# The MLPs' first products as seven products of halves per pair of feature tiles

## The chip, the cores and the metric

The kernel runs on one core of a Trainium2 chip (trn2). The metric is the device time of one execution in microseconds (us), as the median of several runs on the same chip.

## The reference

A decoder trunk of two layers over 1024 tokens of 1024 features, in float32. Layer 0 mixes the tokens with an S5 state-space mixer and a gated linear unit (GLU), layer 1 with a Mamba-2 SSD mixer. After each mixer stands an MLP, which is what changes here. Cut to what matters:

```python
def _sq_relu_mlp(h, w1, w2):          # h [1024, 1024], w1 [1024, 4096], w2 [4096, 1024]
    a = jax.nn.relu(h @ w1)
    return (a * a) @ w2

for i in range(2):
    sh1, sc1, g1, sh2, sc2, g2 = split(silu(c) @ ada_w[i] + ada_b[i])
    x = x + g1 * mixer_i(_modulate(_rmsnorm(x, norm_mix_g[i]), sh1, sc1))
    h = _modulate(_rmsnorm(x, norm_mlp_g[i]), sh2, sc2)       # h * (1 + scale) + shift
    x = x + g2 * _sq_relu_mlp(h, mlp_w1[i], mlp_w2[i])
return _rmsnorm(x, final_norm_g)
```

## The kernel before

Activations lie with the features on the 128 partitions: `x` and `h` are 8 feature tiles of 1024 tokens, each in two halves of 512 tokens (`f` or `half` 0 and 1), so one matmul takes a 128 x 128 block of weights and 512 columns of tokens into one PSUM bank. Every float32 operand of a dense product is split into two parts that float32r holds exactly, `hi` and `lo` (`split`, L80: a cast on ACT, a subtraction on DVE), and a product is three matmuls, hi·hi, hi·lo and lo·hi (`mm3`, L98). A `unit` (L86) is a raw tile of weights of 128 x 1024, loaded by SP's queue, and its split into two stationary tiles; units rotate through a ring of five.

An MLP (`mlp`, L351) goes through the 4096 inner features in 8 groups (`fg`) of 4 feature tiles. In each group the first products are made for 4 tiles and 2 halves (`project`, 24 matmuls each, 192 in all), their squared relu is made by ACT and DVE and split into `ah` and `al`, and then the second products (`accumulate`, L377) run over the 4 tiles for 8 output tiles and 2 halves, 12 matmuls each, 192 in all. Their sums are added to `x`, times the gate, on DVE (L384). So the inner activations of a group never leave SBUF, and `x` stays there through the whole MLP. While layer 0's MLP runs, the modulation vectors of layer 1 are made on DVE, as dot products over 512 KB tiles (`mods`, L296), four steps for each half group.

The norm in front of the MLP works on one half of the tokens at a time (`norm_half`, L184): squares on ACT, their sum on DVE, the sum over partitions and the spreading of 1/rms on PE (L158, L141), then two DVE operations and one ACT operation for each feature tile (L194, L201, L202). The mixers end with the second half of the tokens (`glu` L737 and `ssd_out` L993 call `mid(f)`), so that the norm of the first half runs beside the mixer's matmuls of the second half, and the norm of the second half beside the MLP's products of the first half. In layer 0, `mid` of the MLP itself makes the norm for the SSD mixer, and writes `x` to DRAM (`rscr`).

The code is written out in one order. An instruction takes its place in its engine's queue when its inputs and its buffer are there, and of several such the one that stands first in the text. So work from further down can run ahead where an engine would be idle, if a buffer is free for it. Once the kernel is built, the order in each queue is fixed. Pools of tiles are allocated as two stacks, from the left and from the right; a pool that takes the place of a released one waits tile by tile for the old users.

Of the kernel before, what the change touches and what calls it, by code (L numbers as in the profile page):

```python
# [70 lines left out]
def psw(K):  # L71
    """A bank for the work of a mixer."""
    return K.pw.tile([P, 512], F32, tag="pw", name="pm")
# [6 lines left out]
def split(K, hi, lo, src):  # L80
    """src = hi + lo, each of them exact in float32r."""
    K.nc.scalar.copy(hi, src)  # L82
    K.nc.vector.tensor_tensor(lo, src, hi.bitcast(F32), op=ALU.subtract)  # L83


def unit(K, src, n=1024):  # L86
    """n columns of stationary blocks, split in two."""
    raw = K.raw.tile([P, 1024], F32, tag="raw", name="raw")[:, 0:n]
    K.nc.sync.dma_start(raw, src)
    K.wturn = (K.wturn + 1) % 5  # L90
    wt = K.wt if K.wturn < 2 or not K.wx else K.wx
# [6 lines left out]
def mm3(K, ps, terms, start=True, stop=True):  # L98
    """ps = sum of w^T x over the terms, w and x given as (hi, lo)."""
    n = len(terms)  # L100
    for i, (wh, wl, xh, xl) in enumerate(terms):
        K.nc.tensor.matmul(ps, wh, xh, start=start and i == 0, stop=False)  # L102
        K.nc.tensor.matmul(ps, wh, xl, start=False, stop=False)  # L103
        K.nc.tensor.matmul(ps, wl, xh, start=False, stop=stop and i == n - 1)  # L104
# [11 lines left out]
def rsqrt(K, y, v):  # L116
    """y = v ** -0.5 by Newton's steps from the bits of v."""
# [14 lines left out]
def pss(K):  # L132
    """A bank for the norms."""
# [3 lines left out]
def spread(K, y, bank=pss):  # L137
    """PSUM [P, 512] whose rows are all the 512 values of y [P tokens, 4 chunks]."""
# [6 lines left out]
def rstd_half(K, xs, bank=pss):  # L145
    """1/rms of each of 512 tokens, on all partitions."""
# [37 lines left out]
def norm_half(K, x, h, half, G, sh):  # L184
    """h = x * rstd * G + sh, split, for one half of the tokens."""
# [12 lines left out]
def shift_split(K, t, h, sh):  # L198
    """h = t + sh, split."""
# [5 lines left out]
def h_tile(K, k, half, s, dtype=F32R):  # L205
    """The slot of the h pool for (feature tile, half, hi or lo)."""
# [27 lines left out]
def together(main, other, ratio):  # L234
    """Runs the generator main to its end with ratio steps of the other after each of its own."""
# [23 lines left out]
def mod_setup(K):  # L259
# [32 lines left out]
def mod_dot(K, w, acc):  # L292
    """acc = sum over the free dimension of w times 2 silu(c)."""
    r = K.raw.tile([P, 1024], F32, tag="raw", name="ada")
# [4 lines left out]
def columns(K, rows, n):  # L299
    """PSUM [P, n]: the values of a row, on one partition in two banks, down the partitions."""  # L300
# [10 lines left out]
def mod_shift(K, w):  # L311
    """Shift of the first norm, on the tensor engine."""
# [16 lines left out]
def mod_gate(K, ada, k):  # L329
    """The gate of the first mixer, halved, for feature tile k."""  # L330
# [92 lines left out]
def sines(K, out, t, turn, bias, u):  # L423
    """out = sin(2 pi (t + turn)); t in turns, bias = 2 pi turn, u scratch."""
# [40 lines left out]
    # the angle in turns, in [-1/2, 1/2]  # L465
# [24 lines left out]
    # R[0], R[1]: (cos; sin) and (-sin; cos) of j times the angle, times the magnitude  # L490
# [15 lines left out]
    # the angle of a chunk  # L506
# [5 lines left out]
    # (exp(lambda dt) - 1) / lambda  # L512
# [71 lines left out]
    # the response after 0..7 tokens, (channel in; token, group, channel out)  # L584
# [15 lines left out]
    # token s sees the responses s later: rows of 16 tokens, of which the first 8 are read  # L600
# [22 lines left out]
    # times i, the halves change places  # L623
# [3 lines left out]
    # E holds (re, im, re), so that both (re, im) and (im, re) are in it  # L627
# [25 lines left out]
def s5_uproj(K, h, w):  # L653
    """u = h W_in, stored by feature with the tokens as (token in chunk, chunk)."""
# [16 lines left out]
def s5_main(K, S, G, outp, m):  # L671
    """The recurrence over chunks for 8 groups, and the gelu of its output."""
# [10 lines left out]
    for qd in range(2):  # L683
# [7 lines left out]
        # each chunk's input in the turning frame, and the state after it  # L691
# [678 lines left out]
```

## Time and profile before

| | before |
|---|---|
| median of 3 runs | 2657.85 us (2654.13 to 2659.31) |
| span of the profiled execution | 2655.8 us, 2.05 us below that median |
| PE busy | 2605.1 us, 98% |
| weight loads (PEld) | 2105.9 us, 79% |
| DVE busy | 1577.7 us, 59% |
| ACT busy | 910.1 us, 34% |
| POOL busy | 19.2 us, 1% |
| DMA | 291.86 MB, mean 110 GB/s |
| granted TensorE clock, mean | 0.992 |

The times of the single execution that was profiled are those of its span, from the first to the last instruction. PE is TensorE's matmuls, PEld its loads of weights, DVE VectorE, ACT ScalarE, POOL GpSimd, SP the queue that issues most DMAs. In a row of the timeline the columns are the start in us, the length in us, the engine, the line and the operation, what is written from what, the shape and the count, and in brackets how long the engine sat idle before it and what ended that. In a row of the groups they are the line, engine, operation, shapes and count, then the busy time in us and the mean of one in ns, and the idle time before them. Matmuls are pipelined, so the length of one is more than the distance to the next.

### The profile page before, as it was taken

The page shows a single profiled execution, that of the slowest core. Times are in us where ns is not written, and L with a number is a line of the kernel's source. Part 1 is how long each engine was busy: PE and PEld are TensorE (multiplying, and loading weights), DVE is VectorE, ACT ScalarE, POOL GpSimd, SP SyncE. Part 2 cuts the span into 40 slices and gives each one's busy share as a digit, 9 for nine tenths or more (in the row PEclk, how much of TensorE's full clock was granted, in tenths as well). Part 3 has the DMA queues.
Part 4 walks back from the last instruction along what each step waited for, and adds up shares of the span by engine and source line. Part 5 has one row for each costly group of instructions (what it writes and reads, how often), then busy time and mean ns, then how long its engine had stood idle before and what let it go on. Part 6 is the DMA issues. An engine that isn't in the chain of part 4 may idle for free.

```text
span 2655.8 us, 31465 instructions
## 1 busy us (share of the span) xinstructions
PE 2605.1 (98%) x12392; PEld 2105.9 (79%) x12392; DVE 1577.7 (59%) x2699; ACT 910.1 (34%) x1503; POOL 19.2 (1%) x40
## 2 busy tenths in 40 slices
PE   7999899999999999999999999999999999999997
PEld 2787788888888888877887788778888888888886
DVE  8797657744444433378595968697663333333335
ACT  4577213221122112244464646543332122211221
POOL 0010000000000000000000000000000000000000
PEclk8999999999999999999999999999999999999998
DMA  6576664322222211122455445663111111111101
GB/s 239 151 176 185 222 203 128 102 95 96 96 95 98 93 63 35 65 93 106 152 168 163 152 155 159 207 213 107 40 64 46 50 48 48 48 48 48 48 25 63
DMA packets 156947, 291.86 MB, mean 110 GB/s; under 512 B 12160, under 2 KB 86912, under 8 KB 156800
## 3 DMA queue, kind: packets, MB, share of 16 engines
q1 hardware_dynamic: 143616, 268.89, 30.9%
q0 software_dynamic: 3584, 12.58, 2.5%
q10 hardware_dynamic: 9600, 8.39, 1.0%
q8 instruction: 97, 1.59, 0.2%
q14 instruction: 50, 0.41, 0.0%
HBM read 234.24 MB, written 51.38 MB: 108 GB/s over the span
## 4 chain that ended last, share of the span: by engine, by line
PE 90%; DMA 4%; DVE 3%; ACT 2%; issue 0%; SPq 0%; DVEq 0%; ACTq 0%
PE pd L102 28%; PE pd L103 27%; PE pd L104 27%; PE pm L951 1%; PE pm L711 1%; PE pm L963 1%; PE pm L979 1%; DMA csb<-csr 1%; PE pn L141 1%; DMA yr<-yscr 1%; DMA gfm<-gscr 0%; PE pn L594 0%; PE pm L924 0%; PE pm L709 0%; ACT L L934 0%
## 5 line engine op out<-in xcount | busy, mean ns | idle before, releaser
L82 ACT CAST whi<-raw 128x1024 fp32r<-128x1024 f32 x209 | 218.5, 1046 | 930.2 <-PE pd L103 913.8
L83 DVE TENSOR_TENSOR wlo<-raw,whi 128x1024 fp32r<-128x1024 f32 x209 | 255.0, 1220 | 265.9 <-ACT whi L82 259.3
L104 PE MATMUL pd<-ah,wlo 128*128 128x512 f32 x1024 | 401.8, 392 | 0.0
L103 PE MATMUL pd<-al,whi 128*128 128x512 f32 x1024 | 401.7, 392 | 0.0
L102 PE MATMUL pd<-ah,whi 128*128 128x512 f32 x1024 | 401.5, 392 | 0.0
L384 DVE SCALAR_TENSOR_TENSOR x<-pd,mod,x 128x512 f32<-128x512 f32 x256 | 191.6, 750 | 324.4 <-PE pd L104 324.4
L103 PEld LDWEIGHTS pd<-al,whi 128*128 128x128 f32 x1024 | 192.5, 188 | 42.7
L102 PEld LDWEIGHTS pd<-ah,whi 128*128 128x128 f32 x1024 | 192.4, 188 | 42.6
L104 PEld LDWEIGHTS pd<-ah,wlo 128*128 128x128 f32 x1024 | 192.4, 188 | 42.6
L364 DVE TENSOR_TENSOR sq<-r 128x512 f32<-128x512 f32 x128 | 87.8, 688 | 167.3 <-ACT r L362 167.3
L296 DVE SCALAR_TENSOR_TENSOR ada<-ada,cond 128x1024 f32<-128x1024 f32 x88 | 107.6, 1223 | 94.1 <-DMA ada<-in_ada 93.7
L362 ACT ACTIVATE r<-pd 128x512 f32<-128x512 f32 x128 | 75.9, 593 | 245.9 <-PE pd L104 245.9
L365 DVE TENSOR_TENSOR al<-sq,ah 128x512 fp32r<-128x512 f32 x128 | 88.3, 691 | 12.3
L881 DVE SCALAR_TENSOR_TENSOR cacc<-cr,conv,cacc 128x1024 f32<-128x1024 f32 x72 | 92.0, 1278 | 0.1
L934 ACT ACTIVATE L<-csb,cs 128x128 f32<-128x128 f32 x224 | 69.9, 390 | 36.5 <-DMA csb<-csr 36.4
L363 ACT ACTIVATE ah<-r 128x512 fp32r<-128x512 f32 x128 | 81.0, 633 | 3.9
L102 PE MATMUL pd<-h00h,whi 128*128 128x512 f32 x161 | 65.3, 407 | 2.5 <-ACT h00h L201 1.8
L102 PE MATMUL pd<-h01h,whi 128*128 128x512 f32 x161 | 64.4, 400 | 0.0
L103 PE MATMUL pd<-h00l,whi 128*128 128x512 f32 x161 | 64.3, 399 | 0.1
L104 PE MATMUL pd<-h10h,wlo 128*128 128x512 f32 x161 | 64.3, 399 | 0.0
L103 PE MATMUL pd<-h30l,whi 128*128 128x512 f32 x161 | 63.9, 397 | 0.0
L102 PE MATMUL pd<-h10h,whi 128*128 128x512 f32 x161 | 63.9, 398 | 0.0
(496 smaller groups left out, 5700.6 us busy)
## 6 DMA issues: line engine op xcount, KB each, us to landing
raw<-in_w SPq DMA_DIRECT2D x128, 512.0 KB, 3.2
ada<-in_ada SPq DMA_DIRECT2D x96, 512.0 KB, 3.3
csb<-csr SPq DMA_DIRECT2D x32, 512.0 KB, 4.4
raw<-in_w_xbc SPq DMA_DIRECT2D x24, 512.0 KB, 4.1
xscr<-cacc SPq DMA_DIRECT2D x24, 512.0 KB, 2.7
raw<-in_s_w_glu SPq DMA_DIRECT2D x16, 512.0 KB, 4.6
raw<-in_w_z SPq DMA_DIRECT2D x16, 512.0 KB, 3.8
zscr<-zs SPq DMA_DIRECT2D x32, 256.0 KB, 3.4
```

What stands on the lines that cost most here:

```text
L82: K.nc.scalar.copy(hi, src)
L83: K.nc.vector.tensor_tensor(lo, src, hi.bitcast(F32), op=ALU.subtract)
L102: K.nc.tensor.matmul(ps, wh, xh, start=start and i == 0, stop=False)
L103: K.nc.tensor.matmul(ps, wh, xl, start=False, stop=False)
L104: K.nc.tensor.matmul(ps, wl, xh, start=False, stop=stop and i == n - 1)
L296: K.nc.vector.scalar_tensor_tensor(r, r, 1.0, K.cond, op0=ALU.mult, op1=ALU.mult, accum_out=acc)
L362: nc.scalar.activation(r, p, AF.Relu)
L363: nc.scalar.activation(hi, r, AF.Square)
L364: nc.vector.tensor_tensor(sq, r, r, op=ALU.mult)
L365: nc.vector.tensor_tensor(lo, sq, hi.bitcast(F32), op=ALU.subtract)
L384: K.nc.vector.scalar_tensor_tensor(o, p, gate[:, m:m + 1], x[m][f], op0=ALU.mult, op1=ALU.add)
L881: V.scalar_tensor_tensor(acc, cr[:, t:t + L], K.cw[:, i, t:t + 1], acc, op0=ALU.mult, op1=ALU.add)
```

## The change

The first products of an MLP get a phase of their own, before all second products. Two feature tiles of the inner layer and two halves of tokens, over two halves of the input features, are a product of 2 x 2 by 2 x 2 blocks. It is made with seven products of blocks instead of eight (the Winograd form of Strassen's scheme): 12 matmuls each (4 blocks of 128 features, three matmuls). The sums of weight blocks are made on DVE for each pair (`Up.rest`), the sums of activation blocks once for each MLP (`up_second`: panels T1 to T4, with eight of the subtractions on POOL), and the sums of the seven products partly in PSUM and partly on DVE (`Up.begin`, `Up.end`, `Up.out`). The squared relu goes to DRAM (`ascr`, on POOL's queue) and is read back and split in the second phase (`mlp_down`). The norm writes over `x`, which is therefore saved to DRAM before (`hscr`, on POOL's queue) and read again for the second phase. The panels and the second `x` take the place of part of the weight ring on the left; the ring in the first phase is two slots of `wt`, one of `wy` and two of a new pool `wz`, which lies where `x` was. In a group of the second phase the next group's four tiles of activations are loaded first; then, four times over, a unit of weights and a tile of activations of the next group are split and four `accumulate` follow, with one step of the modulation. `held` is a copy out of PSUM on ACT, `product` twelve matmuls over four blocks. The modulation's tiles of layer 1 come from two buffers in `wz`, two steps for each pair. `ready` is called ahead of the mixer's last update, and `begin` of the first three pairs (`UPS`) is issued at the entry, around the norm of the second half.

```diff
 def rstd_half(K, xs, bank=pss, between=lambda: None):
...
     rsqrt(K, y, v)
+    between()
     return spread(K, y, bank)
...
+def up_norm(K, x, half, G, sh, save, h, order, lows=True, between=lambda: None):
+    nc, V = K.nc, K.nc.vector
+    for k in range(KT):
+        nc.gpsimd.dma_start(save[k, :, half_of(half)], x[k][half])
+    pb = rstd_half(K, [x[k][half] for k in range(KT)], between=between)
+    for k in order:
+        t = x[k][half]
+        V.scalar_tensor_tensor(t, t, G[:, k:k + 1], pb, op0=ALU.mult, op1=ALU.mult)
+        if h[k][half]:
+            nc.scalar.activation(h[k][half][0], t, AF.Identity, bias=sh[:, k:k + 1])
+        V.tensor_scalar(t, t, sh[:, k:k + 1], None, op0=ALU.add)
+        if h[k][half] and lows:
+            up_low(K, h[k][half], t)
+        yield k
+
+def up_low(K, hl, t):
+    K.nc.vector.tensor_tensor(hl[1], t, hl[0].bitcast(F32), op=ALU.subtract)
+
+def up_first(K, x, G, sh, save):
+    h = h_new()
+    h_half(K, h, 0)
+    drain(up_norm(K, x, 0, G, sh, save, h, range(KT)))
+    return SimpleNamespace(b11=[h[k][0] for k in range(4)], b21=[h[4 + k][0] for k in range(4)])
+
+def up_second(K, pan, pool, x, G, sh, save, begin):
...
+    pan.b22 = [h[4 + j][1] for j in range(4)]
+    pan.t1 = [(h_tile(K, j, 1, 0), h_tile(K, j, 1, 1)) for j in range(4)]
+    pan.t2, pan.t3, pan.t4 = panel("t2"), panel("t3"), panel("t4")
+    order = [k for j in range(4) for k in (4 + j, j)]
+    outs = []
+    def between():
+        outs.extend(begin(m) for m in range(1, UPS))
+    outs.append(begin(0))
+    for k in up_norm(K, x, 1, G, sh, save, h, order, False, between):
+        if k < 4:
+            b11, b12, b21, b22 = x[k][0], x[k][1], x[4 + k][0], x[4 + k][1]
+            t2 = tmp(K, "t2")
+            TT(V, b11, b12, b11)
+            TT(V, t2, b22, b11)
+            split(K, *pan.t2[k], t2)
+            TT(nc.gpsimd, b12, b22, b12)
+            TT(nc.gpsimd, b21, b21, t2)
+    outs[0]()
+    for j in range(4):
+        split(K, *pan.t3[j], x[j][1])
+    for o in outs[1:]:
+        o()
+    for j in range(4):
+        split(K, *pan.t1[j], x[j][0])
+    for j in range(4):
+        split(K, *pan.t4[j], x[4 + j][0])
+    for j in range(4):
+        up_low(K, pan.b22[j], x[4 + j][1])
+
+class Up:
...
+    def first(self, m):
+        g = self.g[m] = SimpleNamespace()
+        g.r0 = unit_raw(self.K, self.w1[2 * m])
+        g.u0 = unit_of(self.K, g.r0)
+
+    def rest(self, m, pool):
+        K, V, g = self.K, self.K.nc.vector, self.g[m]
+        r0, r1 = g.r0, unit_raw(K, self.w1[2 * m + 1])
+        g.a22 = tuple(pool.tile([P, HT], F32R, tag="a22" + s, name="a22" + s, bufs=2) for s in "hl")
+        split(K, *g.a22, r1[:, HT:])
+        V.tensor_tensor(r1[:, HT:], r1[:, 0:HT], r1[:, HT:], op=ALU.add)
+        V.tensor_tensor(r1[:, 0:HT], r0[:, 0:HT], r1[:, 0:HT], op=ALU.subtract)
+        V.tensor_tensor(r0[:, 0:HT], r1[:, HT:], r0[:, 0:HT], op=ALU.subtract)
+        g.u2 = unit_of(K, r1)
+        V.tensor_tensor(r0[:, HT:], r0[:, HT:], r0[:, 0:HT], op=ALU.subtract)
+        g.u1 = unit_of(K, r0)
...
+    def out(self, t, m, i, f, p=None):
+        nc = self.K.nc
+        if p is not None:
+            nc.vector.tensor_tensor(t, t, p, op=ALU.add)
+        nc.vector.scalar_tensor_tensor(t, t, 0.0, t, op0=ALU.max, op1=ALU.mult)
+        nc.gpsimd.dma_start(self.ascr[2 * m + i, :, half_of(f)], t)
+
+    def begin(self, m, pan):
+        K, g = self.K, self.g[m]
+        g.X = (K.ps if m % 4 < 2 else K.psb).tile([P, 512], F32, tag="ps", name="px")
+        self.product(g.X, g.u0, 0, pan.b11, True)
+        Z = K.pw.tile([P, 512], F32, tag="pw", name="pz")
+        self.product(Z, g.u0, HT, pan.b21, True)
+        return lambda: self.out(self.held(g.X, "s1"), m, 0, 0, Z)
+
+    def end(self, m, pan):
+        K, g = self.K, self.g.pop(m)
+        X = g.X
+        self.product(X, g.u1, 0, pan.t2, False)
+        s2 = self.held(X, "s2")
+        W = K.pw.tile([P, 512], F32, tag="pw", name="pv")
+        self.product(W, g.u2, 0, pan.t3, True)
+        s7 = self.held(W, "s7")
+        self.product(X, g.u2, HT, pan.t1, False)
+        self.out(s7, m, 1, 1, X)
+        self.product(W, g.a22, 0, pan.t4, False)
+        self.out(s2, m, 1, 0, W)
+        self.product(X, g.u1, HT, pan.b22, False)
+        r = tmp(K, "r")
+        K.nc.scalar.activation(r, X, AF.Relu)
+        self.out(r, m, 0, 1)
+
+def mlp_down(K, pool, x, ascr, w2, gate, mid, extra):
+    def raw_a(fg, i):
+        t = pool.tile([P, L], F32, tag="ar", name="ar", bufs=4)
+        K.nc.sync.dma_start(t, ascr[fg * 4 + i])
+        return t
+    def split_a(fg, i, t):
+        for f in range(2):
+            a[fg][f, i] = tuple(h_tile(K, fg % 2 * 4 + i, f, s) for s in range(2))
+            split(K, *a[fg][f, i], t[:, half_of(f)])
+    a, us = {0: {}}, {0: []}
+    for i in range(4):
+        us[0].append(unit(K, w2[0, i]))
+        split_a(0, i, raw_a(0, i))
+    for fg in range(8):
...
+    def mlp(i, x, xa, up, pan, gate, mid, cond=None, mods=()):
+        K.wz = right("wz" + str(i), 2)
+        unit_ring(K, K.wt, K.wt, K.wy, K.wz, K.wz)
+        for t in ("whi", "wlo"):
+            K.wz.tile([P, 1024], F32R, tag=t, name=t, bufs=2)
+        K.adap = K.wz if cond else None
+        for m in range(UPS):
+            up.rest(m, K.wz)
+            up.end(m, pan)
+            if m == UPS - 1:
+                up.first(UPS)
+                up.rest(UPS, K.wz)
+        for m in range(UPS, 16):
+            up.begin(m, pan)()
+            if m < 15:
+                up.first(m + 1)
+            up.end(m, pan)
+            if m < 15:
+                up.rest(m + 1, K.wz)
+            for _ in range(2):
+                next(mods, None)
+        K.tp.release()
+        xl = left("xl" + str(i))
+        x = x_tiles(xl)
+        for k in range(KT):
+            for f in range(2):
+                nc.sync.dma_start(x[k][f], K.hscr[i][k, :, half_of(f)])
+        ar = right("ar" + str(i))
+        mlp_down(K, ar, x, K.ascr[i], io.w2[i], gate, lambda f: mid(x, f), lambda: next(mods, None))
...
+        def ready():
+            for m in range(UPS):
+                up.first(m)
+        def mid(f):
+            if f == 0:
+                up.pan = up_first(K, x, G, sh, K.hscr[i])
+            else:
+                K.wx.release()
+                K.tp = left("tp" + str(i))
+                up_second(K, up.pan, K.tp, x, G, sh, K.hscr[i], lambda m: up.begin(m, up.pan))
...
-    for _ in mlp(K, ap, x, h, io.w1[0], io.w2[0], modv(K, 0, 5), mid):
-        for _ in range(4):
-            next(mod1, None)
-    drain(mod1)
     xa.release()
-    ap.release()
+    mlp(0, x, xa, up, up.pan, modv(K, 0, 5), mid, True, mod1)
     cond.release()
+    K.wx = left("wx1", 2)
+    unit_ring(K, K.wt, K.wt, K.wx, K.wx, K.wy)
```

More of the change, by code (lines that the diff above doesn't have):

```diff
@@ L86, in unit, with unit_raw, unit_of @@
 def unit(K, src, n=1024):
+    return unit_of(K, unit_raw(K, src, n), n)
+def unit_raw(K, src, n=1024):
     raw = K.raw.tile([P, 1024], F32, tag="raw", name="raw")[:, 0:n]
     K.nc.sync.dma_start(raw, src)
-    K.wturn = (K.wturn + 1) % 5
-    wt = K.wt if K.wturn < 2 or not K.wx else K.wx
+    return raw
+def unit_of(K, raw, n=1024):
+    K.wturn = (K.wturn + 1) % len(K.wring)
+    wt = K.wring[K.wturn]
     hi = wt.tile([P, 1024], F32R, tag="whi", name="whi")[:, 0:n]
@@ L95, in unit, with unit_ring, mm3 @@
     return hi, lo
-def mm3(K, ps, terms, start=True, stop=True):
+def unit_ring(K, *pools):
+    K.wring, K.wturn = list(pools), -1
+def mm3(K, ps, terms, start=True, stop=True, more=False):
     n = len(terms)
     for i, (wh, wl, xh, xl) in enumerate(terms):
-        K.nc.tensor.matmul(ps, wh, xh, start=start and i == 0, stop=False)
-        K.nc.tensor.matmul(ps, wh, xl, start=False, stop=False)
-        K.nc.tensor.matmul(ps, wl, xh, start=False, stop=stop and i == n - 1)
+        K.nc.tensor.matmul(ps, wh, xh, start=start and i == 0, stop=False, skip_group_check=more)
+        K.nc.tensor.matmul(ps, wh, xl, start=False, stop=False, skip_group_check=more)
+        K.nc.tensor.matmul(ps, wl, xh, start=False, stop=stop and i == n - 1, skip_group_check=more)
 def project(K, u, h, half, p=None, ks=range(KT)):
@@ L142, in spread, with rstd_half @@
     return pb
-def rstd_half(K, xs, bank=pss):
+def rstd_half(K, xs, bank=pss, between=lambda: None):
     nc = K.nc
@@ L292, in mod_dot @@
 def mod_dot(K, w, acc):
-    r = K.raw.tile([P, 1024], F32, tag="raw", name="ada")
+    pool, bufs = (K.adap, 2) if K.adap else (K.raw, 4)
+    r = pool.tile([P, 1024], F32, tag="ada" if K.adap else "raw", name="ada", bufs=bufs)
     K.nc.sync.dma_start(r, w)
@@ new lines, in up_low, with TT, panel @@
+def up_low(K, hl, t):
[6 more added lines that the diff above has]
+def up_second(K, pan, pool, x, G, sh, save, begin):
+    nc, V = K.nc, K.nc.vector
+    def TT(e, o, a, b):
+        e.tensor_tensor(o, a, b, op=ALU.subtract)
+    def panel(nm):
+        return [
+            tuple(pool.tile([P, HT], F32R, tag=f"{nm}{j}{s}", name=f"{nm}{j}{s}") for s in "hl") for j in range(4)
+        ]
+    h = h_new()
+    for k in range(4, KT):
+        h[k][1] = (h_tile(K, k, 1, 0), h_tile(K, k, 1, 1))
+    pan.b22 = [h[4 + j][1] for j in range(4)]
[26 more added lines that the diff above has]
+        up_low(K, pan.b22[j], x[4 + j][1])
@@ new lines, with __init__, product, held @@
+class Up:
+    def __init__(self, K, w1, ascr):
+        self.K, self.w1, self.ascr, self.g = K, w1, ascr, {}
+    def first(self, m):
[13 more added lines that the diff above has]
+        g.u1 = unit_of(K, r0)
+    def product(self, p, u, o, panel, start):
+        w = [a[:, o:o + HT] for a in u]
+        mm3(self.K, p, [(w[0][:, blk(j)], w[1][:, blk(j)], *panel[j]) for j in range(4)], start, more=True)
+    def held(self, p, name):
+        t = tmp(self.K, name)
+        self.K.nc.scalar.copy(t, p)
+        return t
[28 more added lines that the diff above has]
+        self.out(r, m, 0, 1)
@@ new lines, in mlp_down @@
+def mlp_down(K, pool, x, ascr, w2, gate, mid, extra):
+    def raw_a(fg, i):
+        t = pool.tile([P, L], F32, tag="ar", name="ar", bufs=4)
+        K.nc.sync.dma_start(t, ascr[fg * 4 + i])
+        return t
+    def split_a(fg, i, t):
[6 more added lines that the diff above has]
+        split_a(0, i, raw_a(0, i))
+    for fg in range(8):
+        last = fg == 7
+        if not last:
+            a[fg + 1], us[fg + 1] = {}, []
+            ahead = [raw_a(fg + 1, i) for i in range(4)]
+        for i in range(4):
+            if last:
+                continue
+            if i > 0:
+                us[fg + 1].append(unit(K, w2[fg + 1, i - 1]))
+            split_a(fg + 1, i, ahead[i])
+            for f in range(2):
+                for m in (2 * i, 2 * i + 1):
+                    accumulate(K, us[fg], a[fg], f, m, x, gate)
+            extra()
+        if last:
+            for f in range(2):
+                for m in range(KT):
+                    accumulate(K, us[fg], a[fg], f, m, x, gate)
@@ L1177, in trunk @@
         p.release()
-    K.wx = tc.alloc_tile_pool(name="wx", bufs=3, side="right", reuse_waits="tile")
+    K.wy, K.wx = left("wy"), left("wx0", 2)
+    unit_ring(K, K.wt, K.wt, K.wx, K.wx, K.wy)
+    K.wturn = 1
     us += glu_units(K, io.s5_w_glu, 1)
@@ L1272, in trunk, with final @@
     drain(outs)
-    def final(f):
-        pb = rstd_half(K, [x1[k][f] for k in range(KT)])
+    xa.release()
+    def final(x, f):
+        pb = rstd_half(K, [x[k][f] for k in range(KT)])
         for k in range(KT):
```

91 lines of the change are left out of this document (44 added, 47 removed).

## The prediction

> **What bounds the kernel now.** First the page's busy times and the windows by stage, then the groups, then the timeline where the change cuts in.
>
> ```profile
> span 2655.8 us, 31465 instructions
> ...
> PE 2605.1 (98%) x12392; PEld 2105.9 (79%) x12392; DVE 1577.7 (59%) x2699; ACT 910.1 (34%) x1503; POOL 19.2 (1%) x40
> ...
> 480.00:1130.00 650.00, 650.00 (x2841) 533.63 (x2840) 303.38 (x409) 143.07 (x196) 0.00 (x0) 1.00 0.25 84
> ...
> 1945.00:2620.00 675.00, 674.95 (x2953) 553.90 (x2952) 263.72 (x341) 147.22 (x203) 0.00 (x0) 1.00 0.13 43
> ```
>
> The last two rows are the two MLPs (start and end, length, busy PE, PEld, DVE, ACT, POOL, granted clock, DMA share, GB/s). PE is busy all the time at full clock, DVE under half, DMA at most a quarter. So a matmul less is time saved, as long as nothing new makes PE wait. What a matmul costs is its spacing, not the 392 ns of its group, since matmuls overlap:
>
> ```profile
> 2157.97 0.75 DVE L384 SCALAR_TENSOR_TENSOR x<-pd,mod,x 128x512 f32<-128x512 f32 x1 [1.46 <-PE pd L104]
> ...
> 2245.82 0.75 DVE L384 SCALAR_TENSOR_TENSOR x<-pd,mod,x 128x512 f32<-128x512 f32 x1 [1.31 <-PE pd L104]
> ```
>
> These are the same update in two successive groups of layer 1, with one group's 384 matmuls between: 87.85 us, 0.2288 us each.
>
> DVE's costs too are distances between starts, read from one unbroken stretch (a row's second column overlaps the next start):
>
> ```profile
> 457.08 1.22 DVE L83 TENSOR_TENSOR wlo<-raw,whi 128x1024 fp32r<-128x1024 f32 x1
> 458.22 0.74 DVE L202 SCALAR_TENSOR_TENSOR h60l<-nt,mod,h60h 128x512 fp32r<-128x512 f32 x1
> 458.88 0.74 DVE L202 SCALAR_TENSOR_TENSOR h70l<-nt,mod,h70h 128x512 fp32r<-128x512 f32 x1
> 459.54 0.74 DVE L756 SCALAR_TENSOR_TENSOR gv<-pd,cst,gt 128x512 f32<-128x512 f32 x1
> 460.21 0.48 DVE L755 TENSOR_SCALAR gt<-gt,g1h 128x512 f32<-128x512 f32 x1
> 460.60 0.68 DVE L757 TENSOR_TENSOR x<-x,gv 128x512 f32<-128x512 f32 x1
> 461.20 0.74 DVE L756 SCALAR_TENSOR_TENSOR gv<-pd,cst,gt 128x512 f32<-128x512 f32 x1
> ```
>
> So 1.14 for two tensors of 1024 columns, and for 512 columns 0.66 (scalar_tensor_tensor), 0.39 (tensor_scalar), 0.60 (tensor_tensor).
>
> **1. The matmuls.** A pair of feature tiles took 2 x 2 x 8 x 3 = 96 matmuls; seven products of four blocks take 7 x 12 = 84. 12 x 16 pairs x 2 layers = 384 fewer, the number of one group: -87.85 us. The second products keep theirs.
>
> **2. The steady first phase.** PE needs 84 x 0.2288 = 19.2 us a pair.
>
> ```profile
> L82 ACT CAST whi<-raw 128x1024 fp32r<-128x1024 f32 x208 | 218.1, 1049 | 930.1 <-PE pd L103 913.8 <-DMA raw<-in_s_w_glu 10.6 <-DMA raw<-in_s_w_in 4.3
> ...
> L861 ACT COPY cr<-pd 128x512 f32<-128x512 f32 x48 | 27.9, 581 | 41.3 <-PE pd L104 41.3
> ...
> L296 DVE SCALAR_TENSOR_TENSOR ada<-ada,cond 128x1024 f32<-128x1024 f32 x88 | 107.6, 1223 | 94.1 <-DMA ada<-in_ada 93.7
> ...
> L626 POOL DMA_DIRECT2D Fb<-Fa x8 | 4.5, 565 | 0.0
> ```
>
> DVE: three low parts of weights (3.42), a22's low part and four sums of weights (3.0), three sums onto products (1.8), four squared relus (2.64), in layer 0 two modulation dots (2.44): 13.3 us. ACT: three casts, a22's, three copies out of PSUM, a relu, about 6.1 us. POOL: four stores, 2.3 us of issue. SP's queue carries two units and two dots. All lie beside PE's 19.2: cost 0, taken. It could be more where a bank is handed over (rival D). In the second phase a group has 192 x 0.2288 = 43.9 us of PE over 16 updates, 4 low parts of weights, 8 of activations and 4 dots, 24.9 us of DVE: 0.
>
> **3. The entry of the phase: the main cost.** Up to now PE had four products of the first half (96 matmuls, 22 us) while the second half was normalised. Now it has begin(0) to begin(2), 72 matmuls or 16.5 us; end(0) needs T2, T3, T1, T4, B22 and the weight sums. Where DVE stands when PE runs out of the mixer's matmuls:
>
> ```profile
> 432.52 0.39 PE L102 MATMUL pd<-h01h,whi 128*128 128x512 f32 x1
> ...
> 467.38 1.22 DVE L296 SCALAR_TENSOR_TENSOR ada<-ada,cond 128x1024 f32<-128x1024 f32 x1
> ...
> 474.89 1.13 PE L141 MATMUL pn<-ident,rsy 128*128 128x128 f32 x8
> ...
> 476.06 2.06 DVE L194 SCALAR_TENSOR_TENSOR nt<-x,G,pn 128x512 f32<-128x512 f32 x3 [1.31 <-PE pn L141]
> ...
> 1930.66 0.75 DVE L384 SCALAR_TENSOR_TENSOR x<-pd,mod,h71l 128x512 f32<-128x512 f32 x1 [0.26 <-PE pd L104]
> ...
> 1943.97 2.07 DVE L194 SCALAR_TENSOR_TENSOR nt<-x,G,pn 128x512 f32<-128x512 f32 x3 [1.31 <-PE pn L141]
> ```
>
> Layer 0: GLU's second half begins at 432.52; 96 matmuls and two small norm steps of 1.1 end at 456.7, the norm of that half starts 19.4 later. Layer 1: 1930.66 to 1943.97, 13.3. The new first half costs DVE 0.66 + 0.39 + 0.60 a tile instead of 2 x 0.66, +2.6; one unit fewer is split ahead, -1.1; in layer 0 two dots (one shown, of layer 1's modulation, issued ahead) move into the phase, -2.4; in layer 1 an out fills in, +1.3. Starts: 18.5 and 16.1 us after PE's last mixer matmul.
>
> From there DVE has: the loop, 4 x (2 x (0.66 + 0.39) + 3 x 0.60) = 15.6; the last out, 1.3; the low parts of T3, T1, T4, B22, 16 x 0.60 = 9.6. Then rest(0): by the diff a22 lies in the memory that x's tiles have just left, so its split waits for the splits of T1 (layer 0) or T4 (layer 1), the sums into r1 wait for a22, and both units for these; being last in the text, they also come after DVE's other work. a22's low part 0.6, three sums 1.8, a cast 1.05, hand-offs 0.3, the low part 1.1: 4.85. Sum 31.4, so end(0) starts at 49.9 and 47.5. PE has 16.5 + 2.2 (norm steps) = 18.7: idle 31.2 + 28.8 = 60 us. Bounds: with the weight sums made in earlier gaps only the pace of DVE counts; the last B22 is then at 18.5 + 26.5 + 0.7 = 45.7 against 18.7 + 13.7 = 32.4, idle 13.3 and 10.9, together 24. Above: rival C. I take 60, since I find no reason for that slot to be free sooner.
>
> **4. The clock after such a gap.**
>
> ```profile
> 250.00:255.00 5.00, 2.03 (x12) 1.42 (x10) 3.14 (x7) 0.60 (x1) 0.00 (x0) 0.96 0.83 274
> 255.00:260.00 5.00, 4.73 (x19) 4.57 (x20) 2.38 (x3) 3.57 (x4) 0.00 (x0) 0.50 0.94 356
> 260.00:265.00 5.00, 5.00 (x31) 4.49 (x31) 5.00 (x6) 5.00 (x5) 0.00 (x0) 0.86 0.48 157
> ```
>
> After 3 idle us the granted clock is 0.50 for 5 us and 0.86 for 5: 3.2 us lost. Two entries: +6.4.
>
> **5. From the first phase to the second.** The weights of w2 are prefetched in free slots. x returns through DRAM, 4.2 MB into the room of T2 and T3, free 10.9 and 8.2 us before PE's end; at the 356 GB/s of the row above 11.8 us. In layer 0 the tiles for `ar` seem to lie on T4's, whose last product ends 2.7 us before the end; three of them (1.6 MB, 4.4 us) queue behind x on SP, and the first product needs all: -10.9 + 11.8 + 4.4 + 1.3 for a split (0.58 + 0.69, the rows above) = 6.6 us late, or 0 if the memory is apart. I take 5; layer 1, with a smaller wz, 0. x's saves (POOL's queue) are 300 us old by then; at the entry they stand before the in-place norm:
>
> ```profile
> Fb<-Fa POOLq DMA_DIRECT2D x16, 256.0 KB, 7.0
> ...
> raw<-in_w SPq DMA_DIRECT2D x128, 512.0 KB, 3.2
> ```
>
> 7 us of landing lie inside the 16 to 18 before the loop: 0.
>
> **6. SSD's start.** Its ring now partly lies on x's old tiles:
>
> ```profile
> 1165.14 0.75 DVE L384 SCALAR_TENSOR_TENSOR x<-pd,mod,x 128x512 f32<-128x512 f32 x1 [0.23 <-PE pd L104]
> ...
> 1168.01 0.51 DVE L83 TENSOR_TENSOR wlo<-raw,whi 128x256 fp32r<-128x256 f32 x1
> ...
> 1177.84 2.06 DVE L194 SCALAR_TENSOR_TENSOR nt<-x,G,pn 128x512 f32<-128x512 f32 x3 [1.31 <-PE pn L141]
> ```
>
> The split at 1168.01 (the third unit) now waits until x's tiles 0 to 2 are normalised, 1179.9; PE has 48 matmuls (11 us) and 2.2 from 1165.1, to 1178.3. Between 0 and 3, taken 2.5.
>
> **Sum.** -87.85 + 60 + 6.4 + 5 + 2.5 = -14 us. From the profiled 2655.8: 2642; the median of the runs lies 2.05 above that span: 2644. From here on 0.2% (5.3 us) is what a measurement can tell.
>
> **Rivals.**
>
> A, the sum: 2644, its own range 2630 to 2656.
>
> B, the entry is mostly hidden: rest(0) finds its buffer early, or DVE's lows are ordered as PE wants them. Idle 24 instead of 60: 2608. For it: dots of layer 1 run at 467.38, long before their place in the text, so free work does move forward. Against: a22's slot, which can't be free before x's tiles are.
>
> C, POOL's eight subtractions in the loop hold DVE back. No row has one; the nearest are
>
> ```profile
> L783 POOL TENSOR_SCALAR_AFFINE_SELECT tri<-tri 128x128 f32<-128x128 f32 x1 | 0.7, 682 | 919.9 <-issue 919.9
> ...
> masks.py:199 POOL TENSOR_SCALAR_AFFINE_SELECT ident<-ident 128x128 f32<-128x128 f32 x1 | 0.3, 288 | 0.0
> ```
>
> for a quarter of the columns: four times that is 1.15 to 2.73 us each. Beside DVE they end in time to within 4 us (8 x 2.73 from 3.9 into the loop, T4 wanted at 21.7). If each stops DVE while it runs, the loop is 9.2 to 21.8 longer a layer: 2662 to 2687. For it: nothing in the trace, where POOL never computes beside DVE. [...]
>
> D, slower by the banks: in end(), X is read by DVE's add between t1's and b22's product, and PE has one product, 12 x 0.2288 = 2.75 us, before it writes X again. The add takes 0.69; behind one op of 1.22 it fits, behind two it doesn't. At 70% DVE in layer 0 that can happen. It decides from 14 / 32 = 0.44 us a pair; at 1.2 us the time is 2682. Against: DVE takes the earliest in the text first, and the add precedes the next pair's weights.
>
> That the products aren't fewer is no rival: PE's count shows in the diff.
>
> **Chances.** A 0.50, B 0.20, C 0.17, D 0.13. Faster by over 0.2% (below 2652.5): most of A (0.43) and B, 0.63. Within: 0.06 of A and 0.05 of C, 0.11. Slower: 0.12 of C, D and 0.01 of A, 0.26. The range reaches from B's price with the smaller terms gone, 2605, to C's and D's upper part, 2684, with one in ten left out at each end.
>
> **What would show it.** Matmuls 384 fewer; a gap of some 30 us on PE after the third begin in each layer, ended by a unit's cast or low part (A), or 11 to 13 in pieces (B); a clock of 0.5 behind it; DVE's subtractions longer than 0.69 while POOL computes (C); PE waits between products of one pair, ended by DVE's sums onto s7 (D); a wait for `ar` at the start of layer 0's second phase. The forecast is wrong above all if a22's place isn't what I read.

## The result, and the profile after

The changed kernel takes 2679.77 us (median of 4 runs, 2677.76 to 2681.49), the kernel before 2658.3 beside it: ratio 1.0083, 95% interval 1.0069 to 1.0097. It is 22 us slower, where 14 us less were forecast. Its profiled execution has a span of 2676.1 us, 20.3 more than that of before.

The page's busy times and the windows by stage of the changed kernel; the two windows are those shown of before:

```profile
span 2676.1 us, 32145 instructions
...
PE 2519.0 (94%) x12008; PEld 2035.5 (76%) x12008; DVE 1809.5 (68%) x3059; ACT 976.1 (36%) x1591; POOL 129.4 (5%) x216
...
480.00:1130.00 650.00, 594.96 (x2569) 486.38 (x2570) 409.39 (x575) 172.17 (x236) 43.08 (x70) 0.96 0.44 148
1945.00:2620.00 675.00, 636.18 (x2793) 524.15 (x2791) 394.82 (x537) 187.26 (x256) 50.15 (x79) 0.97 0.31 106
```

The 384 matmuls are gone (12392 to 12008), and PE's busy time fell by 86.1 us. But inside the MLPs, where PE had no idle time before, 55 us of the first window and 39 us of the second are empty now, and the granted clock is below 1.00. PE's waits (waiting instruction, what ended the wait, us in total, times, longest):

```profile
PE pv L116 <- ACT whi L83: 77.1, 2, 38.6
PE pd L116 <- ACT h00h L83: 16.0, 1, 16.0
...
PE px L116 <- DVE s L485: 7.7, 4, 2.6
```

The first row is the entry of the phase, 38.6 us in each layer, the second the start of layer 0's second phase. The third is the banks: PE may not write a bank again before DVE has added the product in it onto s; all four are in layer 0's first phase. The entry of layer 0 in the timelines of PE, DVE and POOL:

```profile
470.63 1.13 PE L155 MATMUL pn<-ident,rsy 128*128 128x128 f32 x8 [0.60 <-DVE rsy L142]
510.36 0.80 PE L116 MATMUL pv<-t30h,whi 128*128 128x512 f32 x1 [38.60 <-ACT whi L83]
```

```profile
471.79 2.06 DVE L375 SCALAR_TENSOR_TENSOR x<-x,G,pn 128x512 f32<-128x512 f32 x3 [1.31 <-PE pn L155]
...
476.82 1.49 DVE L378 TENSOR_SCALAR x<-x,mod 128x512 f32<-128x512 f32 x1
478.23 0.73 DVE L375 SCALAR_TENSOR_TENSOR x<-x,G,pn 128x512 f32<-128x512 f32 x1
...
488.84 1.75 DVE L84 TENSOR_TENSOR t30l<-x,t30h 128x512 fp32r<-128x512 f32 x1
...
497.47 1.27 DVE L485 TENSOR_TENSOR s<-s,pz 128x512 f32<-128x512 f32 x2
498.66 1.28 DVE L486 SCALAR_TENSOR_TENSOR s<-s 128x512 f32<-128x512 f32 x2
...
507.09 0.69 DVE L84 TENSOR_TENSOR a22l<-raw,a22h 128x512 fp32r<-128x512 f32 x1
...
509.26 0.69 DVE L467 TENSOR_TENSOR raw<-raw 128x512 f32<-128x512 f32 x1
```

```profile
476.05 1.98 POOL L402 TENSOR_TENSOR x<-x,x 128x512 f32<-128x512 f32 x1 [14.38 <-issue]
477.99 1.44 POOL L402 TENSOR_TENSOR x<-x,t 128x512 f32<-128x512 f32 x1
...
488.60 1.44 POOL L402 TENSOR_TENSOR x<-x,t 128x512 f32<-128x512 f32 x1 [0.63 <-DVE t L402]
```

PE has nothing left after the norm's spreading; DVE then works from 471.79 on with three short waits for ACT (0.26, 0.16 and 0.34 us), and rest(0)'s a22 and sums stand last, behind all the panels, as the prediction had it; the unit's cast ends PE's wait. What its sum did not have is in the stretched rows. The operation at 476.82 takes 1.49 us instead of 0.48 while POOL subtracts, and that at 488.84, 1.75 instead of 0.68: it starts 0.24 after POOL's subtraction, and ends at 490.59, 0.55 after that one's end (490.04). The one at 478.23 has its second input in PSUM (pn) and keeps its 0.73 beside POOL's.

The clock after each gap, in windows (start and end, length, busy PE, PEld, DVE, ACT, POOL, granted clock, DMA share, GB/s):

```profile
510.30:540.00 29.70, 28.71 (x111) 22.66 (x112) 26.58 (x39) 10.70 (x15) 1.62 (x3) 0.88 0.72 233
2013.80:2040.00 26.20, 25.90 (x103) 20.59 (x104) 19.48 (x25) 10.01 (x13) 1.62 (x3) 0.90 0.51 165
832.00:850.00 18.00, 18.00 (x66) 14.38 (x67) 14.60 (x22) 9.44 (x16) 0.00 (x0) 0.83 0.82 280
...
1130.00:1260.00 130.00, 126.86 (x562) 98.06 (x561) 93.53 (x183) 48.02 (x71) 0.60 (x1) 0.99 0.26 90
```

111 matmuls of 0.2288 are 25.4 us and took 28.7; 103 are 23.6 and took 25.9; 66 are 15.1 and took 18.0. The three recoveries cost 8.5 us. The last row is the start of SSD: 3.1 us idle, where the kernel before has 0.3 in the same stretch (its 1110 to 1240), so 2.8 more. Its 562 matmuls took 126.9 us; at the pace of the kernel before there (583 in 129.7 us) they would take 125.0. That is 1.9 us more, with a granted clock of 0.94 between 1200 and 1230.

The start of the second phase in layer 0, in the timelines of PE, of SP's queue and of ACT:

```profile
804.54 0.39 PE L118 MATMUL px<-t23h,wlo 128*128 128x512 f32 x1
...
815.53 0.39 PE L118 MATMUL px<-h71h,wlo 128*128 128x512 f32 x1
831.93 0.80 PE L116 MATMUL pd<-h00h,whi 128*128 128x512 f32 x1 [16.02 <-ACT h00h L83]
```

```profile
780.63 32.80 SPq L94 DMA_DIRECT2D raw<-in_w  x6
813.52 11.41 SPq L1304 DMA_DIRECT2D x<-hscr  x16
...
831.26 0.62 ACT L83 CAST h00h<-ar 128x512 fp32r<-128x512 f32 x1 [13.99 <-DMA ar<-ascr]
```

T2 is used for the last time at 804.54 and the phase's last matmul starts at 815.53. The loads of x stand behind loads of weights that wait for a buffer until 813.5, some 8.6 us after T2's room was free; the tiles of `ar` come behind x, and PE starts at 831.93.

### The profile page after: what moved, and what is told of

Read it like the earlier page. It is cut to its first block, busy times and chain, and to the rows that moved or that the text cites. A ratio compares the mean times of both kernels' runs of the same rounds, so it can differ in the third digit from the quotient of the medians.

```text
span 2676.1 us, 32145 instructions
## 1 busy us (share of the span) xinstructions
PE 2519.0 (94%) x12008; PEld 2035.5 (76%) x12008; DVE 1809.5 (68%) x3059; ACT 976.1 (36%) x1591; POOL 129.4 (5%) x216
## 5 line engine op out<-in xcount | busy, mean ns | idle before, releaser
L83 ACT CAST whi<-raw 128x1024 fp32r<-128x1024 f32 x241 | 252.1, 1048 | 708.2 <-PE pd L117 529.0
L84 DVE TENSOR_TENSOR wlo<-raw,whi 128x1024 fp32r<-128x1024 f32 x241 | 293.1, 1218 | 93.7 <-ACT whi L83 88.4
L485 DVE TENSOR_TENSOR s<-s,px 128x512 f32<-128x512 f32 x32 | 22.0, 686 | 107.3 <-issue 102.3
L116 PE MATMUL pv<-t30h,whi 128*128 128x512 f32 x32 | 13.3, 416 | 77.1 <-ACT whi L83 77.1
L487 POOL DMA_DIRECT2D ascr<-s x96 | 51.8, 540 | 500.1 <-DVE s L486 488.2
L486 DVE SCALAR_TENSOR_TENSOR s<-s 128x512 f32<-128x512 f32 x96 | 65.9, 688 | 1.6
L371 POOL DMA_DIRECT2D hscr<-x x32 | 17.4, 543 | 967.0 <-DVE x L563 755.0
L118 PE MATMUL pd<-h00h,wlo 128*128 128x512 f32 x161 | 63.7, 396 | 0.0
L117 PE MATMUL pd<-h10l,whi 128*128 128x512 f32 x161 | 63.6, 395 | 0.0
L116 PE MATMUL pd<-h20h,whi 128*128 128x512 f32 x161 | 63.6, 395 | 0.0
L116 PE MATMUL pd<-h21h,whi 128*128 128x512 f32 x161 | 63.5, 394 | 0.0
```

Source lines behind the costliest of these rows:

```text
L117: K.nc.tensor.matmul(ps, wh, xl, start=False, stop=False, skip_group_check=more)
L485: nc.vector.tensor_tensor(t, t, p, op=ALU.add)
L486: nc.vector.scalar_tensor_tensor(t, t, 0.0, t, op0=ALU.max, op1=ALU.mult)
L487: nc.gpsimd.dma_start(self.ascr[2 * m + i, :, half_of(f)], t)
```

## The experiments

All edits are to the changed kernel, and each time is a median beside runs of the kernel before on the same chip. The theory was that the entry is as long as DVE's stretch, and that the losses at the other two places are separate and add up.

**POOL's subtractions cut short.**

```diff
-            TT(nc.gpsimd, b12, b22, b12)
-            TT(nc.gpsimd, b21, b21, t2)
+            TT(nc.gpsimd, b12[:, 0:32], b22[:, 0:32], b12[:, 0:32])
+            TT(nc.gpsimd, b21[:, 0:32], b21[:, 0:32], t2[:, 0:32])
```

> The eight subtractions on POOL are cut to the first 32 of their 512 columns, in both layers; the rest of the panels T3 and T4 is left unsubtracted. The order on every engine is that of the changed kernel. Theory (the subtractions hold DVE back, and the entry lasts as long as DVE's work): DVE's operations between POOL's fall back to 0.48 and 0.68 us, the 38.6 us gap on PE in front of the first product with T3 shrinks by about 5.3 us in each layer, the time falls by 10.6 us, from 2679.8 to 2669. Rival (POOL computes beside DVE at no cost, and the stretched rows have another cause, a wait for ACT's casts): the gap stays at 38.6 and the time at 2680.

Measured: 2674.51 us, ratio to before 1.0064 (1.0049 to 1.0079), some 5 us less than the changed kernel; the two intervals overlap, so the reading rests on the trace. Waits of PE, the same two DVE operations, a later wait of DVE and one of POOL's subtractions in this run:

```profile
PE pv L116 <- ACT whi L83: 69.9, 2, 34.9
```

```profile
481.32 0.48 DVE L378 TENSOR_SCALAR x<-x,mod 128x512 f32<-128x512 f32 x1
...
489.96 0.68 DVE L84 TENSOR_TENSOR t30l<-x,t30h 128x512 fp32r<-128x512 f32 x1
...
495.44 0.69 DVE L485 TENSOR_TENSOR s<-s,pz 128x512 f32<-128x512 f32 x1 [1.80 <-ACT s L478]
```

```profile
489.72 4.04 POOL L402 TENSOR_TENSOR x<-x,t 128x32 f32<-128x32 f32 x1 [1.01 <-DVE t L402]
```

The stretching is POOL's doing. The gap is 3.6 us shorter in a layer, not the 5.3 expected, because POOL is still in the way: its sixth subtraction, now of 32 columns, took 4.04 us, where twelve of the sixteen took 0.25 to 0.43. It ended at 493.76, just behind a run of DVE's tensor_tensors that lasted until 493.65, so here DVE held POOL up. A cast on ACT waited 3.50 us for it, and DVE 1.80 for the copy behind that cast.

**The subtractions on DVE.**

```diff
-            TT(nc.gpsimd, b12, b22, b12)
-            TT(nc.gpsimd, b21, b21, t2)
+            TT(V, b12, b22, b12)
+            TT(V, b21, b21, t2)
```

> The eight subtractions are made by DVE instead of POOL. Theory (POOL's subtractions exclude DVE's): eight more operations of 0.60 us, 4.8 us a layer, against 5.3 us of stretching that is gone: the gap on PE stays within 1.5 us of 38.6 and the time within 3 us of 2680. Rival (POOL's work beside DVE costs nothing): the gap grows by 4.8 us in each layer, time 2689.

Measured: 2679.57 us, ratio 1.0082 (1.0067 to 1.0097), and in PE's waits of this run:

```profile
PE pv L116 <- ACT whi L83: 74.0, 2, 37.0
```

Eight operations more on DVE make each gap 1.6 us shorter, and DVE has no wait for ACT left in its stretch. They are 8 x 0.60 = 4.8 us of work, so without them the gap would be 32.2, and on POOL they cost it 6.4 us in a layer (an estimate from this run and the changed kernel). It is part of the 38.6, not most of it. Moving them to POOL had gained nothing; the time is the same.

**x's loads on another queue.**

```diff
-                nc.sync.dma_start(x[k][f], K.hscr[i][k, :, half_of(f)])
+                nc.gpsimd.dma_start(x[k][f], K.hscr[i][k, :, half_of(f)])
```

> The sixteen loads of x at the start of the second phase are issued on POOL's queue instead of SP's. Theory (on SP they stood behind a load of weights that waited for a buffer until 813.2, 8.4 us after T2 was free): they start at about 805 in layer 0, the loads of ar at about 813, and PE's gap of 16.0 us shrinks to 3 to 5 us, with the half clock behind it gone: 13 to 15 us less, 2666. Rival (the room of ar lies on T4, or the two transfers need their 16 us of DMA anyway): the gap stays above 12 us, time 2676 to 2680.

Measured: 2673.02 us (2666.41 to 2676.26), ratio 1.0058 (1.0038 to 1.0078); the profiled execution is that of 2669.88 us. PE's wait in it, and POOL's queue in front of x's loads:

```profile
PE pd L116 <- ACT h00h L83: 6.3, 1, 6.3
```

```profile
811.59 0.54 POOL L487 DMA_DIRECT2D ascr<-s  x1 [7.70 <-DVE s L486]
812.12 1.10 POOL L1304 DMA_DIRECT2D x<-hscr  x2
```

The gap is 9.7 us shorter, but not because x comes earlier, as the theory had it: on POOL's queue x's loads stand behind a store that waits for DVE until 811.59, and start at 812.12 instead of 813.52. What changed is that `ar` no longer stands behind x: its loads start at 812.89 instead of 825.30, right after the last product with T4 (812.14). What stays is the time until the first tile of `ar` has landed (its cast starts at 820.93), on a DMA that it shares with x, as a window of this run shows (its last two columns are the DMA share and the GB/s):

```profile
820.00:825.00 5.00, 3.40 (x8) 2.73 (x9) 2.28 (x4) 2.27 (x4) 0.92 (x2) 0.50 1.03 406
```

Of the 13 to 15 us expected, 6.8 are seen in the time.

**The dots later, first attempt.**

```diff
-            for _ in range(2):
-                next(mods, None)
...
-        mlp_down(K, ar, x, K.ascr[i], io.w2[i], gate, lambda f: mid(x, f), lambda: next(mods, None))
+        mlp_down(K, ar, x, K.ascr[i], io.w2[i], gate, lambda f: mid(x, f), lambda: (next(mods, None), next(mods, None)))
```

> The modulation's dot products of layer 1 are taken out of the first phase of layer 0 and made in the second phase, two a step instead of one. Theory (in layer 0 DVE is late for the sum onto s because dots and low parts of weights stand ahead of it): the four waits of PE px for DVE s, 7.7 us, are gone, the second phase has room (4 dots of 1.22 more for each group, 29.8 of 43.9 us), time 2672. Rival (the second half of the dots makes the second phase wait, or the waits have another cause): 2680 or more.

Measured: 2682.25 us, ratio 1.0094 (1.0079 to 1.0109), and the same four waits, 8.9 us. But the edit changed nothing: 48 dots lie between 510 and 800 us in this run as in the changed kernel. As their buffers are free, the dots ran in the first phase all the same, ahead of their place in the text. A row of DVE and one of PE in this run, with what they waited for:

```profile
677.85 1.22 DVE L312 SCALAR_TENSOR_TENSOR ada<-ada,cond 128x1024 f32<-128x1024 f32 x1 [3.12 <-DMA ada<-in_ada]
```

```profile
679.73 0.50 PE L116 MATMUL px<-h41h,whi 128*128 128x512 f32 x1 [2.67 <-DVE s L485]
```

The sum onto s stands right behind this dot on DVE, at 679.00, and PE waits for the sum. So the theory changed: not DVE's load is at fault, but a dot whose transfer has not landed, with the sum behind it in a fixed order.

**The dots later, in fact.** As before, and their tiles lie in the second phase's pool:

```diff
-        K.adap = K.wz if cond else None
...
         ar = right("ar" + str(i))
+        K.adap = ar if cond else None
```

> The dot products' tiles now lie in the second phase's pool, so that no dot of layer 1's modulation can run in the first phase of layer 0 (but the few before the entry); two a step in the second phase. Theory (D's waits come from a dot that waits for its own transfer, 3.10 us in the row at 677.06, while it stands ahead of the sum onto s in DVE's order): the four waits of PE px for DVE s, 7.7 us, are gone, the 16.0 us at the start of the second phase stay, time 2672. Rival (DVE is late for the sum because of low parts of weights, not of dots): at least 5 us of these waits stay, time 2677 or more.

Measured: 2668.45 us, ratio 1.0044 (1.003 to 1.0058). No wait of PE px for DVE s is left in the first phase; the other two stay, in PE's waits:

```profile
PE pv L116 <- ACT whi L83: 77.1, 2, 38.6
PE pd L116 <- ACT h00h L83: 16.5, 1, 16.5
```

The time is some 11 us below that of the changed kernel, where 7.7 were expected; what the rest is, these waits do not show.

**Plain products at the entry.** The first two pairs of each layer are made as before the change, which gives PE 192 matmuls that need no panel: `plain` is a `project` of 24 matmuls, with the relu and the square on ACT, for four feature tiles and both halves. The panels come only then, in place of the old ring, with all sixteen subtractions on DVE. The core of the edit:

```diff
+    h_half(K, h, 1)
+    up_norm(K, x, 1, G, sh, save, h)
+    for f in range(2):
+        for t in range(2 * UPS):
+            up.plain(t, f, h)
+    pool = tp()
...
+    out = up.begin(UPS, pan)
```

> In each layer the first two pairs are made as plain products of 8 feature tiles (96 matmuls each instead of 84), both halves, while DVE makes the panels; the subtractions are all on DVE, the norm's shift is added by ACT, and the low parts of b22 come with the norm. Theory (the gap is DVE's work of 38 us with 18.7 us of PE work to cover it, so it closes when PE has work that needs no panel): 48 matmuls more, +11.0; the 77.1 us of gaps fall to 0 to 8 in both layers; two recoveries of the clock are gone, -6; time 2614, between 2604 and 2625. Rival (the gap comes from the chain of weight sums behind a22's slot, which starts only when x's tiles are free): at least 15 us stay in each layer, time 2640 or more.

Measured: 2623.94 us, ratio 0.9874 (0.9859 to 0.9889), at the upper end of what was expected. PE's waits in this run:

```profile
PE pd L117 <- ACT h00h L84: 15.9, 1, 15.9
PE px L117 <- ACT whi L84: 11.9, 2, 7.5
...
PE px L119 <- DVE wlo L85: 4.8, 2, 3.3
```

Of 77.1 us 16.7 are left, 8.9 and 7.7 in a layer, where 0 to 8 were expected. So most of the gap was a lack of work for PE; the price is 11.0 us of extra matmuls. The norm's shift is on ACT here and the subtractions are on DVE, so this run is not about the cover alone.

**All of it together.** The plain entry, the dots in the second phase, and

```diff
+        raws = [ar_load(K, ar, K.ascr[i], t, nc.gpsimd) for t in range(4)]
...
-                nc.sync.dma_start(x[k][f], K.hscr[i][k, :, half_of(f)])
+                nc.gpsimd.dma_start(x[k][f], K.hscr[i][k, :, half_of(f)])
```

> The plain entry, the dots in the second phase, and at the start of the second phase the first four loads of ar and those of x on POOL's queue, ar first, with T2 placed so that ar lies on it and T3 and T4 under x. Theory (the losses are separate and add up: entry, sums late behind dots, second phase's start): of the 16.0 us 0 to 3 stay, the 7.7 are gone, the clock recovers once less, time 2614 - 13 - 3 - 8 = 2590, between 2580 and 2602. Rival (what the entry and the dots free is given back, since DVE has all of it to do later): 2610 or more.

Measured: 2603.67 us, ratio 0.9799 (0.9784 to 0.9813): 20 us less than with the entry alone, where 24 were expected. To within 4 us the losses do add up. In PE's waits the entry is now first, and the second phase's start is fifth:

```profile
PE px L117 <- ACT whi L84: 12.6, 2, 8.1
...
PE pd L117 <- ACT h00h L84: 3.4, 1, 3.4
```

**a22's place**, in the changed kernel again:

```diff
+                K.a0 = left("a0" + str(i))
+                up.a22(0, K.a0)
                 up_second(K, up.pan, K.tp, x, G, sh, K.hscr[i], lambda m: up.begin(m, up.pan))
```

> a22 of the first pair gets 4 KB a partition of its own between T4 and the new weight tiles, and its split and the three sums behind it are issued before the norm of the second half; both units still wait for their places on x's old tiles. Theory (the gap is as long as all of DVE's work, and only what leaves the stretch shortens it): 0.6 + 1.8 us of DVE and the hand-offs between them leave, the gaps shrink by 2.5 to 4 us each, time 2673. Rival (B: it was a22's slot that put the first pair's end behind everything, so with the slot free in time only the pace of DVE counts): the gaps shrink to 24 us for both layers together, time 2630.

Measured: 2671.84 us, ratio 1.0054 (1.0037 to 1.0071). The time is what the theory gave, the way there is not. PE's first waits in layer 0, and the one of layer 1:

```profile
491.44 0.80 PE L116 MATMUL px<-t20h,whi 128*128 128x512 f32 x1 [21.25 <-ACT s L485]
493.78 0.80 PE L116 MATMUL pv<-t30h,whi 128*128 128x512 f32 x1 [1.12 <-DVE s L492]
507.96 0.79 PE L118 MATMUL px<-t20h,wlo 128*128 128x512 f32 x1 [9.51 <-DVE wlo L84]
...
528.52 0.79 PE L116 MATMUL pv<-t30h,whi 128*128 128x512 f32 x1 [7.41 <-ACT whi L83]
```

```profile
1998.01 0.79 PE L116 MATMUL px<-t20h,whi 128*128 128x512 f32 x1 [22.25 <-ACT s L485]
```

In layer 1 the gap is 27 us with its smaller pieces, 11 less than before; in layer 0 the pieces sum to 40, as much as before, since there the units' low parts and the second pair come late instead. Neither side had this split. Rival B's 24 us for both layers together are not reached by freeing that slot alone.

**The same place in the combined version.** The weight units' ring has another order here too.

```diff
     out = up.begin(UPS, pan)
+    unit_ring(K, K.wy, K.wt)
+    K.a0 = K.tc.alloc_tile_pool(name="a0" + str(pool.name)[-1], bufs=1, reuse_waits="tile")
+    up.rest(UPS, K.a0, 1)
```

> The version with the plain entry, the dots later and the loads on POOL's queue, and in it the weight sums of the first seven-product pair in memory of their own, issued ahead of the panels. Theory (in that version DVE stood idle for 4.2 us at 489.6 and was full from 498 until PE's gap of 8.9 us in layer 0; sums moved into idle time leave the full stretch): the gaps of 8.9 and 7.9 us shrink by 4 to 5 us each, time 2603.7 - 9 - 1 = 2594. Rival (the gaps come from T1, whose tiles wait for the last plain product on PE): they stay, time 2603.

Measured: 2585.92 us (2583.62 to 2589.37), ratio 0.973 (0.9716 to 0.9745). The entry of layer 0 and that of layer 1 in windows, and PE's waits in the first of them:

```profile
440.00:535.00 95.00, 92.67 (x416) 75.47 (x415) 86.16 (x141) 61.42 (x96) 8.08 (x15) 1.00 0.35 117
1900.00:2010.00 110.00, 109.21 (x486) 89.62 (x486) 85.09 (x131) 53.86 (x82) 13.70 (x26) 1.00 0.38 130
```

```profile
PE px L117 <- ACT s L481: 2.1, 2, 1.3
```

The gaps of 8.9 and 7.9 us are gone and the clock stays at 1.00: 18 us less, nearly twice what was expected, since the gaps closed altogether. With the other order of the ring, this is not a22's place alone. This version is 2.7% faster than the kernel before and 94 us faster than the changed one.

**The spreading first.** One step moved in the text. It changes PE's order in layer 1 only; in layer 0, as the row at 470.63 shows, PE has run out of other work and waits 0.60 us for 1/rms:

```diff
-    between()
-    return spread(K, y, bank)
+    pb = spread(K, y, bank)
+    return between() or pb
```

> Only the place of one step in PE's order is changed: in layer 1 the spreading of 1/rms of the second half now stands near the start of the third begin's matmuls instead of behind them (layer 0 has it in front already). Theory (the gap is DVE's stretch from that spread on, less PE's work that is left): DVE's norm starts 4.2 us earlier in layer 1, at about 1971, PE's gap there falls from 38.5 to about 34, layer 0 is unchanged, time 4 us less than the changed kernel run beside it. Rival (DVE's start does not count, since rest(0) ends on something else): the gap's end stays and the time is the same.

> The changed kernel once more, beside the others on this chip: 2680, ratio to the kernel before 1.008, from both theories.

Measured: 2678.8 us (2672.87 to 2683.9) against 2679.3 (2678.29 to 2681.79) for the changed kernel beside it; ratios to before 1.0084 (1.007 to 1.0099) and 1.0082 (1.0068 to 1.0096). PE's waits, and DVE's norm in layer 1:

```profile
PE pv L116 <- ACT whi L83: 72.6, 2, 38.6
```

```profile
1970.36 2.07 DVE L375 SCALAR_TENSOR_TENSOR x<-x,G,pn 128x512 f32<-128x512 f32 x3 [1.31 <-PE pn L155]
```

The gap of layer 1 fell to 34.0, 4.5 less, as the theory had it. The trace is that of the fastest run, 2672.87 us. In the time these runs scatter over 11 us, so a gain of 4 is neither shown nor excluded by it.

## Why the prediction was wrong

| step | forecast, us | measured, us |
|---|---|---|
| 1, matmuls | -87.85 | 384 fewer, as forecast |
| 2, steady first phase (rival D) | 0 | 7.7, layer 0 alone |
| 3, entry | 60 | 77.1 |
| 4, clock | 6.4 | 8.5 after three gaps, 1.9 at SSD's start |
| 5, second phase's start | 5 | 16.0 |
| 6, SSD's start | 2.5 | 2.8 |
| sum | -14 | +26, against +20.3 in the spans |

Rival A's mechanism was right, and its size was not. Steps 3, 5 and 2 are the terms that failed, by 17.1, 11.0 and 7.7 us, so that a gain became a loss; the clock adds 4.0 and step 6 0.3. Of the 6 us by which the measured terms overshoot the spans, 4.3 lie ahead of all this: DVE's norm of the second half starts at 471.79, in the kernel before at 476.06. That is mostly scatter, as it starts at 476.29 and 476.94 in the first two experiments, with the same code up to there.

*Step 3.* Cover, order and end of the gap came as forecast. DVE's stretch was sized at 31.4 us and took 38.6 in layer 0. Six operations beside POOL's subtractions are 5.3 us longer than they are without, and the three waits for ACT, 0.8 us, stand behind casts that wait for POOL; the sum had nothing for either, and both are gone with the subtractions on DVE. Two more outs lie inside the stretch (the rows at 497.47 and 498.66), where I had counted one; that is 2.4. On the other side, rest(0) took 3.3 us from 507.09 on instead of 4.85: its cast starts beside the third sum, and PE does not wait for the low part. That leaves 0.3. Layer 1 lost 2.3 more than layer 0 against the forecast, because the spreading stood behind begin's matmuls in PE's order, while I had let DVE start as soon as 1/rms was there; the last experiment gets that and 2.2 more back in the gap.

*Rival C.* I priced it as an alternative to A at 9.2 us a layer and more, and gave it 0.17. It holds beside A, and costs 6.4 (the second experiment). In the trace a tensor_tensor with two inputs in SBUF at 488.84 took 1.75 us instead of 0.68 and ended 0.55 after POOL's subtraction, and an operation with an input in PSUM at 478.23 took its 0.73 beside another. My price was too high because not every subtraction lengthened an operation of DVE: the eight took 12.0 us in layer 0, and six operations became 5.3 longer in all. POOL's took 1.26 to 1.98 us in layer 0, within the bounds of 1.15 and 2.73 that I had taken from two rows of before.

*Step 5.* The three tiles of `ar` on T4's room were read rightly. The step failed in letting x's loads start 10.9 us before PE's end. SP's queue holds loads of weights ahead of them, which wait until 813.5, 2.4 us before that end; I had moved the loads to a queue and not asked what is queued there. With these 8.5 us the step's own sum of 6.6 becomes 15.1 of the measured 16.0. Moving x to POOL's queue did not test this term, since a store stood in front of x there; what that run shows is that 9.7 of the 16.0 go when `ar` does not stand behind x.

*Step 6* came as forecast, 2.8 us for 2.5. That the clock sinks there too was in no step.

*Step 2.* Rival D came true, at 7.7 us instead of the 38 that it had with it, and by another cause than two operations ahead of the sum: a dot that waits for its transfer. The first attempt to move the dots did not separate these, the second did.

A, C, D and the upper bound of step 5 were kept as cases that exclude each other. They are four places, and their prices add. Taken together they would have given a time above 2652.5, so slower or the same, where 0.63 was given to faster.

Freeing a22's slot helps layer 1 by 11 us and layer 0 not at all. The trace of that run shows where layer 0 loses it again. The first unit's low part stands on DVE behind the low parts of all panels and a dot, until 506.69 (the wait of 9.51). And the second pair's weights stand on SP's queue behind nine loads for layer 1's modulation, until 517.07, so that their a22 can be cast only at 525.44 (most of the wait of 7.41); in layer 1 there are no such loads. No run takes them away, so this is read from the rows and not tested.

## What to carry to other kernels

A saving in matmuls is worth its full price only where PE has work while the operands of the new scheme are made: count the cover at the entry, and where it is short, start with the old scheme for a few tiles. Two plain pairs a layer cost 11 us of matmuls and, with the subtractions on DVE and the norm's shift on ACT, took away 60 us of idle time and part of the slow clock behind it (0.985 on average, 0.974 in the changed kernel). Costs at different places add up; don't weigh them as rivals of each other. And before a transfer is put on a queue, read which instruction stands in front of it there and what that one waits for (here loads of weights on SP's, a store on POOL's); the same goes for an operation on DVE whose data come by DMA.

## What the runs showed of the hardware that was not expected

In layer 0 six DVE operations beside POOL's subtractions did not end before the subtraction had, two of them tensor_scalars with one tensor as input: the one at 476.82 took 1.49 us instead of 0.48 and ended 0.28 after the subtraction (478.31 and 478.03). With short subtractions the same operation takes 0.48 again. It goes the other way too: a subtraction of 32 columns took 4.04 us beside DVE's tensor_tensors, where most took 0.25 to 0.43. On balance eight subtractions on POOL, 1.26 to 1.98 us each, made PE's gap 1.6 us longer a layer than the same eight on DVE at 0.60.
